# Attention's second product in one accumulation per pair of heads instead of one per query block

## The chip, the cores and the metric

The kernel runs on one core of a Trainium2 chip. The metric is the time of one execution on the device in microseconds. Three runs of the kernel before the change took 866.69, 867.77 and 871.31 us; their median is 867.77.

The engines are named as in the profile: PE is the matrix engine, PEld its weight loads, DVE the vector engine, ACT the scalar engine, POOL the general-purpose one, SP the queue that issues most DMAs.

## The reference

One layer of a hybrid trunk over 16 learned tokens and 512 input tokens of width 1024. A combined projection feeds an RWKV-7 recurrence (8 heads), a forgetting attention (8 heads, "FoX") and two gates; the two branches are gated, projected and added, and an MLP with squared ReLU follows. The change concerns the attention alone, cut here to what matters:

```python
def block(i):                                    # 128 queries
    logits = einsum('bqhd,bkhd->bhqk', qb, k) * HEAD_DIM ** -0.5
    logits = logits + (Fq[..., None] - F[:, :, None, :])     # F: running sum of log forget gates
    p = softmax(where(kpos <= qpos, logits, -inf), axis=-1)
    return einsum('bhqk,bkhd->bqhd', p, v)       # the second product
```

## The kernel before, in words

The span has three stages. To about 413 us the input projection runs in float32 parts (L501, tiles `pj`), with the recurrence and the attention beside it. From about 440 us come the output projections (L1054, L1086, L1103), then the MLP (L1133, L1251).

In the first stage several generators share PE. PE's instructions are placed in the order in which the generators issue them; a planner (`Turns`, with estimated times from `Clock`) asks each generator at every `yield` when it could go on, and lets the first by rank go that is ready. The chain of the recurrence has rank 0, the rest of the recurrence 1, `attention` 2, `fox_features` (which makes q, k, v of a pair) 3, group norm 4, and the projections, which fill what is left, 8. The other engines' instructions are ordered by a list scheduler from the dependences and from the order of the program.

`attention` takes the heads by pairs p = 0 to 3; the heads e = 0, 1 of a pair lie in the partitions 0 to 63 and 64 to 127 (`hss`). The 512 queries come in four blocks i of 128, and block i looks at the 16 meta keys and at key blocks j = 0 to i. Three steps are made for a block:

- `scored(i)`: scores on PE into PSUM (tiles `psc`, L607), mask and minimum on DVE (L616, L618), exponential with row sum on ACT (L621), division on DVE (L622, L623). The result is `pe`, queries in the partitions.
- `turned(i)`: PE transposes `pe` by key block into PSUM (`ppt`, and `ppm` for the meta keys at i = 3; L636, L638), DVE copies the key blocks to SBUF (`pT`, L640), ACT the meta keys (`pTm`, L641).
- `mixed(i)`: the second product. For each head a matmul over the meta keys (L649) opens the accumulation in the PSUM tile `py`, and one over each key block j up to i (L652) goes on with it, each with 128 queries as moving columns and 64 output rows; ACT copies the 128 x 128 result to `y_fx` (L653).

They go in the order turned(i), scored(i + 1), mixed(i). The PSUM tiles `psc`, `ppt`, `ppm`, `py` and those of the other generators take turns in four banks (`sm`). After the first stage `y_rw` (the recurrence's output) and `y_fx` are split in two float32r parts (`yhi` by ACT, `ylo` by DVE, L270 and L271), one split for each pair p, and L1054 takes them up; its PSUM pool takes over the banks of the first stage.

[...]

Of the kernel before, what the change touches and what calls it, by code (L numbers as in the profile page):

```python
# [9 lines left out]
F32 = mybir.dt.float32  # L10
# [11 lines left out]
S = 512  # L22
# [164 lines left out]
def kernel(ctx, tc, ht, x, win, par, cst, gain, lora, wout, wo, wup, wdn, out, dbg=None):  # L187
    nc = tc.nc
    dbg = dbg or {}
    mm = nc.tensor.matmul  # L190
    act = nc.scalar.activation
    V, G, A = nc.vector, nc.gpsimd, nc.scalar
# [87 lines left out]
    with ExitStack() as st:  # L280
# [8 lines left out]
        def psm(name="psm"):  # L289
            return ps.tile([128, 512], F32, name=name, tag="sm", bufs=4)  # L290
# [42 lines left out]
        with tc.tile_pool(name="xp", bufs=2) as xp:  # L333
# [14 lines left out]
            for t in range(2):  # L348
# [13 lines left out]
                n = 0  # L362
# [40 lines left out]
        y_fx = yp.tile([128, 4, S], F32, name="y_fx")  # L403
# [17 lines left out]
        fp = st.enter_context(tc.tile_pool(name="fp", bufs=1))  # L421
# [3 lines left out]
        ck = Clock(nc)  # L425
# [3 lines left out]
        def banks(n):  # L429
            return ck.ring("sm", n, 4)  # L430
# [155 lines left out]
        def attention():  # L586
            for p in range(4):
                yield fox_ready[p]
                q, k, vt, vm = fox_tiles[p]


                along = []
                for e in range(2):
                    nF = fp.tile([128, T], F32, name=f"nF{e}")
                    nc.sync.dma_start(nF, fF_d[2 * p + e:2 * p + e + 1, :].to_broadcast([128, T]))
                    along.append(nF)

                def scored(i):

                    n = NM + 128 * (i + 1)  # L600
                    parts = [(0, n)] if n <= 512 else [(0, n - 256), (n - 256, n)]
                    yield lambda: max(ck.ready(q, k), banks(2 * len(parts)))
                    scs = [[], []]
                    for a, b in parts:
                        for e, hs in enumerate(hss):
                            sc = psm("psc")[:, :b - a]
                            mm(sc, q[hs, 128 * i:128 * i + 128], k[hs, a:b], start=True, stop=True)  # L607
                            scs[e].append((sc, a, b))
                    pes = []
                    for e in range(2):  # L610
                        pe = fp.tile([128, T], F32, name="pe", bufs=2)
                        nm = fp.tile([128, 2], F32, name="nm", bufs=3)
                        least = 3e38
                        for x, (sc, a, b) in enumerate(scs[e]):
                            if b == n:
                                V.tensor_tensor(sc[:, b - a - 128:], sc[:, b - a - 128:], cmask, ALU.add)  # L616

                            V.tensor_tensor_reduce(pe[:, a:b], sc, along[e][:, a:b], -1.0, least, ALU.add, ALU.min, nm[:, x:x + 1])  # L618
                            least = nm[:, x:x + 1]
                        rsum = fp.tile([128, 1], F32, name="rsum", bufs=3)  # L620
                        act(pe[:, :n], pe[:, :n], AF.Exp, bias=least, scale=-1.0, accum_out=rsum)  # L621
                        V.reciprocal(rsum, rsum)  # L622
                        V.tensor_scalar(pe[:, :n], pe[:, :n], rsum, None, ALU.mult)  # L623
                        pes.append(pe)
                    return pes

                def turned(i, pes):

                    pTs = []
                    pTm = fp.tile([48, 128], F32, name="pTm")  # L630
                    for e in range(2):
                        pe, m = pes[e], slice(32 * e, 32 * e + 16)
                        yield lambda: max(ck.ready(pe), banks(1 + i // 3))
                        pt = psm("ppt")
                        ptm = pt[:16, 384:] if i < 3 else psm("ppm")[:16, :128]
                        nc.tensor.transpose(ptm, pe[:, :NM], ident)  # L636
                        for j in range(i + 1):
                            nc.tensor.transpose(pt[:, 128 * j:128 * j + 128], pe[:, NM + 128 * j:NM + 128 * j + 128], ident)  # L638
                        pT = fp.tile([128, 4, 128], F32, name="pT", bufs=2)
                        V.tensor_copy(pT[:, :i + 1, :].rearrange("p a b -> p (a b)"), pt[:, :128 * (i + 1)])  # L640
                        A.copy(pTm[m], ptm)  # L641
                        pTs.append((pT, pTm[m]))
                    return pTs

                def mixed(i, pTs):
                    yield lambda: max(ck.ready(vt, vm, *pTs[0], *pTs[1]), banks(1))
                    py = psm("py")[:, :128]
                    for e, hs in enumerate(hss):
                        mm(py[hs], vm[32 * e:32 * e + 16, hs], pTs[e][1], start=True, stop=False)  # L649
                    for j in range(i + 1):  # L650
                        for e, hs in enumerate(hss):
                            mm(py[hs], vt[:, j, hs], pTs[e][0][:, j, :], start=False, stop=j == i)  # L652
                    A.copy(y_fx[:, p, 128 * i:128 * i + 128], py)  # L653

                pes = yield from scored(0)
                for i in range(4):
                    pTs = yield from turned(i, pes)
                    if i < 3:
                        pes = yield from scored(i + 1)
                    yield from mixed(i, pTs)  # L660
                fox_done[p].done = True


# [345 lines left out]

        turns.add(1, recurrent())  # L1010
        turns.add(2, attention())
        turns.add(3, fox_features())
        turns.add(8, projections(24 + 16))
# [17 lines left out]
    def ppd():  # L1031
        return ps.tile([128, 512], F32, name="pd")

    with ExitStack() as st:
# [8 lines left out]
        for m in range(KB):  # L1043
            w = ahead.pop() if ahead else load_w(wout[m])
            pp = []
            for br in range(2):
# [4 lines left out]
                n = 0  # L1051
# [46 lines left out]
        for i in range(4):  # L1098
            po = ppo()
            n = 0  # L1100
# [13 lines left out]
            for j in range(2):  # L1114
                cols, kk = slice(512 * j, 512 * j + 512), slice(4 * j, 4 * j + 4)
                V.scalar_tensor_tensor(xt[:, cols], hr[:, cols], ss, gB[:, cols], ALU.mult, ALU.mult)
                pt = ppd().rearrange("p (b c) -> p b c", c=128)
# [264 lines left out]
```

## Time and profile before

| | |
|---|---|
| runs | 866.69, 867.77, 871.31 us |
| median of the runs | 867.77 us |
| profiled execution | span 866.9 us from the first to the last instruction; no longer time of this execution is listed |
| PE busy | 845.5 us in 6040 matmul passes |
| second product on PE | L652: 160 passes, 13.4 us; L649: 64 passes, 7.5 us |
| its copy on ACT | L653: 16, 4.1 us |
| mean granted clock | 0.994 |

An fp32 matmul stands as two passes in the profile, so the 112 matmuls of the second product are 224 passes. Busy times on PE add up passes that overlap: two passes on different column halves run at the same time. The distance from one group's start to the next one's start is the better measure of what a group costs, and the clock column says how much of full speed PE had.

### The profile page before, as it was taken

The page shows a single profiled execution, that of the slowest core. Times are in us where ns is not written, and L with a number is a line of the kernel's source. Part 1 is how long each engine was busy: PE and PEld are TensorE (multiplying, and loading weights), DVE is VectorE, ACT ScalarE, POOL GpSimd, SP SyncE. Part 2 cuts the span into 40 slices and gives each one's busy share as a digit, 9 for nine tenths or more (in the row PEclk, how much of TensorE's full clock was granted, in tenths as well). Part 3 has the DMA queues.
Part 4 walks back from the last instruction along what each step waited for, and adds up shares of the span by engine and source line. Part 5 has one row for each costly group of instructions (what it writes and reads, how often), then busy time and mean ns, then how long its engine had stood idle before and what let it go on. Part 6 is the DMA issues. An engine that isn't in the chain of part 4 may idle for free.

```text
span 866.9 us, 15869 instructions
## 1 busy us (share of the span) xinstructions
PE 845.5 (98%) x6040; PEld 690.8 (80%) x6040; DVE 618.4 (71%) x1222; ACT 458.0 (53%) x943; POOL 123.9 (14%) x129
## 2 busy tenths in 40 slices
PE   7899999999999999999799999999999999999998
PEld 5888887678987877778578878888888888888886
DVE  6986786658786775655767564777678777768687
ACT  7766434856566334663645453474445435534452
POOL 1112100101010000000012100202710360055000
PEclk9999999999999999999989999999999999999999
DMA  6131222121121231312356451551753184336331
GB/s 221 51 98 50 74 83 87 51 72 56 50 74 44 105 116 62 101 37 74 128 180 210 151 159 37 186 181 48 232 168 110 51 251 141 92 114 204 108 98 73
DMA packets 51340, 95.91 MB, mean 111 GB/s; under 512 B 5816, under 2 KB 6968, under 8 KB 51264
## 3 DMA queue, kind: packets, MB, share of 16 engines
q1 hardware_dynamic: 47680, 86.52, 31.8%
q0 software_dynamic: 1280, 4.20, 1.6%
q10 hardware_dynamic: 2304, 4.20, 1.3%
q8 instruction: 47, 0.77, 0.4%
q14 instruction: 29, 0.24, 0.1%
HBM read 88.57 MB, written 6.31 MB: 109 GB/s over the span
## 4 chain that ended last, share of the span: by engine, by line
PE 83%; DVE 5%; ACT 4%; DMA 2%; issue 1%; POOL 0%; ACTq 0%; DVEq 0%; POOLq 0%
PE pj L501 26%; PE po L1133 20%; PE po L1251 11%; PE pd L1251 5%; PE po L1054 3%; PE pw L841 2%; PE po L1103 2%; PE psc L607 1%; PE py L652 1%; PE psr L788 1%; PE pbt L796 1%; DMA wraw<-in_wo 1%; PE ppt L638 1%; DMA gl<-gd 1%; PE pssq L553 1%
## 5 line engine op out<-in xcount | busy, mean ns | idle before, releaser
L501 PE MATMUL pj<-uhi,whi 128*128 128x264 f32 (+1 forms) x480 | 164.9, 343 | 0.0
L501 PE MATMUL pj<-ulo,whi 128*128 128x264 f32 (+1 forms) x480 | 155.1, 323 | 2.5 <-DVE ulo L401 2.5
L501 PE MATMUL pj<-uhi,wlo 128*128 128x264 f32 (+1 forms) x480 | 154.7, 322 | 0.0
L501 PEld LDWEIGHTS pj<-uhi,whi 128*128 128x128 f32 x480 | 90.9, 189 | 17.1 <-issue 8.0
L501 PEld LDWEIGHTS pj<-ulo,whi 128*128 128x128 f32 x480 | 91.2, 190 | 7.4 <-DVE ulo L401 3.0
L501 PEld LDWEIGHTS pj<-uhi,wlo 128*128 128x128 f32 x480 | 91.1, 190 | 7.0
L1133 PE MATMUL po<-zhi,whi 128*128 128x512 f32 (+1 forms) x248 | 94.9, 383 | 0.3 <-ACT whi L235 0.3
L1133 PE MATMUL po<-zhi,wlo 128*128 128x512 f32 (+1 forms) x248 | 94.9, 383 | 0.0
L1133 PE MATMUL po<-zlo,whi 128*128 128x512 f32 (+1 forms) x248 | 94.8, 382 | 0.0
L236 DVE TENSOR_TENSOR wlo<-wraw,whi 128x512 fp32r<-128x512 f32 x88 | 72.5, 836 | 30.1 <-ACT whi L235 30.0
L235 ACT CAST whi<-wraw 128x512 fp32r<-128x512 f32 x88 | 53.7, 617 | 50.7 <-PE po L1133 23.1
L471 DVE TENSOR_TENSOR wlo<-wraw,whi 128x512 fp32r<-128x512 f32 x80 | 55.9, 705 | 25.1 <-ACT whi L470 24.3
L470 ACT CAST whi<-wraw 128x512 fp32r<-128x512 f32 x80 | 48.9, 618 | 40.6 <-PE pj L501 31.6
L270 ACT CAST whi<-t 128x512 fp32r<-128x512 f32 x64 | 39.9, 624 | 44.5 <-DVE wlo L271 20.6
L1251 PE MATMUL po<-wlo,fhi 128*128 128x512 f32 x160 | 62.8, 392 | 0.2 <-DVE wlo L271 0.2
L271 DVE TENSOR_TENSOR wlo<-t,whi 128x512 fp32r<-128x512 f32 x64 | 49.3, 784 | 19.0 <-ACT whi L270 18.1
L1251 PE MATMUL po<-whi,flo 128*128 128x512 f32 x160 | 62.4, 390 | 0.0
L1251 PE MATMUL po<-whi,fhi 128*128 128x512 f32 x160 | 61.9, 389 | 0.0
L1179 POOL TENSOR_TENSOR t<-traw 128x512 f32<-128x512 f32 x24 | 34.3, 1433 | 155.2 <-DVE wlo L271 137.9
L1133 PEld LDWEIGHTS po<-zhi,whi 128*128 128x128 f32 x248 | 46.6, 188 | 9.7 <-ACT whi L235 0.8
L1133 PEld LDWEIGHTS po<-zhi,wlo 128*128 128x128 f32 x248 | 46.6, 188 | 9.4 <-DVE wlo L236 0.4
L1133 PEld LDWEIGHTS po<-zlo,whi 128*128 128x128 f32 x248 | 46.6, 188 | 9.0
(306 smaller groups left out, 1774.6 us busy)
## 6 DMA issues: line engine op xcount, KB each, us to landing
wraw<-in_win SPq DMA_DIRECT2D x84, 256.0 KB, 2.7
wraw<-in_wup SPq DMA_DIRECT2D x64, 256.0 KB, 3.2
wraw<-in_wdn SPq DMA_DIRECT2D x48, 256.0 KB, 2.7
traw<-in_wdn SPq DMA_DIRECT2D x48, 256.0 KB, 3.0
gd<-gt ACTq DMA_DIRECT2D x16, 256.0 KB, 2.1
wraw<-in_wout SPq DMA_DIRECT2D x16, 256.0 KB, 3.1
gl<-gd SPq DMA_DIRECT2D x16, 256.0 KB, 2.8
wraw<-in_wo SPq DMA_DIRECT2D x16, 256.0 KB, 3.0
```

What stands on the lines that cost most here:

```text
L235: A.copy(hi, raw)
L236: low.tensor_tensor(lo, raw, hi.bitcast(F32), ALU.subtract)
L270: A.copy(hi, x)
L271: V.tensor_tensor(lo, x, hi.bitcast(F32), ALU.subtract)
L470: A.copy(hi, raw)
L471: low.tensor_tensor(lo, raw, hi.bitcast(F32), ALU.subtract)
L501: mm(po, a, b[:, k, a0:a1], start=n == 0, stop=n == 23)
L841: mm(ps_[hs, n - b0, :], lhs(n)[hs], rhs(n)[hs], start=True, stop=True)
L1054: mm(po, a, b[:, k, :], start=n == 0, stop=n == 11)
L1133: mm(po[:, t0:t1], a, b[:, k, t0:t1], start=n == 0, stop=n == 23)
L1179: eng.tensor_tensor(t, sums[c, pair] if c in (T1, T2) else c, d, ALU.add)
L1251: mm(x[i], a[:, k, left, 128 * i:128 * i + 128], c, start=start and k == 0 and n == 0, stop=stop and k == n_pairs - 1 and n == 2)
```

## The change

The second product is no longer made for each query block. `turned(i)` stores its transposed key blocks in a buffer that lasts for the whole pair: `pT[e]` has ten places of 128 columns, in an order that puts all queries that look at one key block side by side. Key block 0 has places 0 to 3 (queries 0 to 3), key block 1 places 4 to 6, key block 2 places 8 and 9, key block 3 place 7. The places of one query block are three apart, so DVE writes up to three of them with one strided copy; at i = 3 the fourth is copied by ACT. The meta keys go to `pTm`, which now has 512 columns.

`mixed()` runs once a pair, after `turned(3)`: for each head one matmul over the meta keys with 512 columns, then one for each key block with 512, 384, 256 and 128 columns, all into one PSUM tile, and one ACT copy of 128 x 512. It yields once behind key block 0. A pair has 10 matmuls instead of 28, with as many columns in all. [...]

```diff
+                pT = [fp.tile([128, 10, 128], F32, name=f"pT{e}") for e in range(2)]
+                pTm = fp.tile([48, S], F32, name="pTm")
...
                 def turned(i, pes):
-                    pTs = []
-                    pTm = fp.tile([48, 128], F32, name="pTm")
...
-                        pT = fp.tile([128, 4, 128], F32, name="pT", bufs=2)
-                        V.tensor_copy(pT[:, :i + 1, :].rearrange("p a b -> p (a b)"), pt[:, :128 * (i + 1)])
-                        A.copy(pTm[m], ptm)
-                        pTs.append((pT, pTm[m]))
-                    return pTs
+                        pt = pt.rearrange("p (a b) -> p a b", b=128)
+                        n = min(i + 1, 3)
+                        V.tensor_copy(pT[e][:, i:i + 3 * n - 2:3, :], pt[:, :n, :])
+                        A.copy(pTm[m, 128 * i:128 * i + 128], ptm)
+                        if i == 3:
+                            A.copy(pT[e][:, 7, :], pt[:, 3, :])
 
-                def mixed(i, pTs):
-                    yield lambda: max(ck.ready(vt, vm, *pTs[0], *pTs[1]), banks(1))
-                    py = psm("py")[:, :128]
+                def mixed():
+                    yield lambda: max(ck.ready(vt, vm, pTm, *pT), banks(1))
+                    py = psm("py")
                     for e, hs in enumerate(hss):
-                        mm(py[hs], vm[32 * e:32 * e + 16, hs], pTs[e][1], start=True, stop=False)
-                    for j in range(i + 1):
+                        mm(py[hs], vm[32 * e:32 * e + 16, hs], pTm[32 * e:32 * e + 16, :], start=True, stop=False)
+                    for j, at in enumerate((0, 4, 8, 7)):
                         for e, hs in enumerate(hss):
-                            mm(py[hs], vt[:, j, hs], pTs[e][0][:, j, :], start=False, stop=j == i)
-                    A.copy(y_fx[:, p, 128 * i:128 * i + 128], py)
+                            mm(py[hs, 128 * j:], vt[:, j, hs], pT[e][:, at:at + 4 - j, :].rearrange("p a b -> p (a b)"), start=False, stop=j == 3)
+                        if j == 0:
+                            yield lambda: 0.0
+                    A.copy(y_fx[:, p, :], py)
 
                 for i in range(4):
-                    pTs = yield from turned(i, pes)
+                    yield from turned(i, pes)
                     if i < 3:
                         pes = yield from scored(i + 1)
-                    yield from mixed(i, pTs)
+                yield from mixed()
...
-    nc = bacc.Bacc("TRN2", target_bir_lowering=False, num_devices=1)
+    nc = bacc.Bacc("TRN2", target_bir_lowering=False, num_devices=1, dynamic_dma_scratch_size=8192)
```

Lines move with it: the meta-key matmul L649 becomes L651, the key-block matmul L652 becomes L654, the copy L653 becomes L657, the scores L607 become L609, the exponential L621 becomes L623, the output projection L1054 becomes L1058.

What the order of the instructions shows, at three places. On PE, in the first pair, before: the block of i = 3 among the steps of the recurrence's chain (`pch`, `pyy`, `pvt`).

```order
908 L907 MATMUL pch<-Rs,Tt 64x64 x4
909 L887 MATMUL pvt<-cs,ov 128x64 x2
910 L649 MATMUL py<-pTm,vm 64x128 x2
911 L652 MATMUL py<-pT,vt 64x128 x8
912 L922 MATMUL pch<-uv,bkT 64x64 x4
```

After, in the same pair:

```order
895 L651 MATMUL py<-pTm,vm 64x512 x2
896 L654 MATMUL py<-pT_1502,vt 64x512
897 L654 MATMUL py<-pT_1503,vt 64x512
898 L905 MATMUL pch<-uv,L_703 64x64
899 L905 MATMUL pch<-uv,L_704 64x64
900 L905 MATMUL pch<-uv,L_1121 64x64
901 L905 MATMUL pch<-uv,L_1122 64x64
902 L654 MATMUL py<-pT_1502,vt 64x384
903 L654 MATMUL py<-pT_1503,vt 64x384
904 L654 MATMUL py<-pT_1502,vt 64x256
905 L654 MATMUL py<-pT_1503,vt 64x256
906 L654 MATMUL py<-pT_1502,vt 64x128
```

The one block of the pair is cut in two by a step of the chain; the blocks of i = 0 to 2 further up are gone. The second and third pair are cut in the same way, by L841 and by L922 to L933; the fourth is not cut.

On PE, at the end of the first stage, fourth pair, before:

```order
2160 L649 MATMUL py<-pTm,vm 64x128 x2
2161 L652 MATMUL py<-pT,vt 64x128 x6
2162 L636 MATMUL ppm<-cs,pe 16x128
2163 L638 MATMUL ppt<-cs,pe 128x128 x4
2164 L636 MATMUL ppm<-cs,pe 16x128
2165 L638 MATMUL ppt<-cs,pe 128x128 x4
2166 L649 MATMUL py<-pTm,vm 64x128 x2
2167 L652 MATMUL py<-pT,vt 64x128 x8
2168 L1054 MATMUL po<-yhi,whi 128x512
```

After:

```order
2161 L636 MATMUL ppm<-cs,pe 16x128
2162 L638 MATMUL ppt<-cs,pe 128x128 x4
2163 L651 MATMUL py<-pTm,vm 64x512 x2
2164 L654 MATMUL py<-pT_5255,vt 64x512
2165 L654 MATMUL py<-pT_5256,vt 64x512
2166 L654 MATMUL py<-pT_5255,vt 64x384
2167 L654 MATMUL py<-pT_5256,vt 64x384
2168 L654 MATMUL py<-pT_5255,vt 64x256
2169 L654 MATMUL py<-pT_5256,vt 64x256
2170 L654 MATMUL py<-pT_5255,vt 64x128
2171 L654 MATMUL py<-pT_5256,vt 64x128
2172 L1058 MATMUL po<-yhi,whi 128x512
```

The three earlier blocks have left the places between the transposes, and the whole pair's product stands between the last transpose and the next stage.

On ACT, at the same place, before (casts of `y_rw` and `y_fx`, and the exponential of 528 columns, which is that of i = 3):

```order
418 L641 COPY pTm<-ppt 16x128
419 L270 CAST yhi<-y_rw 128x512 x2
420 L641 COPY pTm<-ppt 16x128
421 L270 CAST yhi<-y_rw 128x512 x2
422 L270 CAST yhi<-y_fx 128x512
423 L621 ACTIVATE pe,rsum<-pe,nm 128x528 x2
424 L653 COPY y_fx<-py 128x128
425 L270 CAST yhi<-y_fx 128x512 x2
```

After:

```order
414 L270 CAST yhi<-y_rw 128x512 x2
415 L642 COPY pTm<-ppt 16x128
416 L270 CAST yhi<-y_rw 128x512 x2
417 L642 COPY pTm<-ppt 16x128
418 L270 CAST yhi<-y_fx 128x512 x3
419 L623 ACTIVATE pe,rsum<-pe,nm 128x528 x2
420 L642 COPY pTm<-ppm 16x128 x2
421 L644 COPY pT_5255<-ppt 128x128
422 L644 COPY pT_5256<-ppt 128x128
423 L657 COPY y_fx<-py 128x512
```

Two more casts stand ahead of the last exponential, and two copies of the fourth key block behind it. On DVE, four splits of `y_rw` stand ahead of the last division (L623 before, L625 after) in both kernels, and one of `y_fx` only after.

## The prediction

> **What bounds the kernel now.** I read the page first, then stretches of the span, then the chain of waits and the timeline around the second product.
>
> ```profile
> span 866.9 us, 15869 instructions
> ...
> 115.00:413.00 298.00, 296.54 (x3094) 235.57 (x3093) 201.26 (x533) 161.59 (x406) 13.86 (x18) 1.00 0.23 73
> 413.00:434.00 21.00, 16.11 (x113) 10.46 (x111) 17.35 (x62) 15.66 (x45) 0.00 (x0) 1.00 0.41 141
> 434.00:442.00 8.00, 7.18 (x37) 5.43 (x38) 4.91 (x10) 2.21 (x7) 0.00 (x0) 0.57 0.43 159
> ```
>
> The last three rows are stretches: start and end, length, busy time of PE, PEld, DVE, ACT and POOL, then the granted clock. Attention for the first three pairs lies in 115 to 413 us, where PE is idle for 1.5 of 298 us: projections (L501) fill every gap, so PE time taken out there should shorten the span one for one. The fourth pair lies in 413 to 440 us. The projections run out there, PE is idle a quarter of the time, and from 434 us the clock falls to 0.57. There the path is a chain, read from the chain of waits (start, length, what):
>
> ```profile
> 428.40 1.38 PE psc L607 x5
> ...
> 430.48 1.66 ACT yhi L270 x3
> 432.14 0.74 ACT pe L621 x2
> ...
> 433.06 0.59 DVE ylo L271
> ...
> 434.13 0.59 DVE ylo L271
> ...
> 436.42 0.62 PE py L649 x4
> ...
> 439.21 0.27 ACT y_fx L653
> ...
> 439.53 6.67 PE po L1054 x24
> ```
>
> The last block's exponential (L621) starts behind casts of y_rw and y_fx that stand ahead of it on ACT, DVE splits stand between its steps, and the next stage (L1054) waits for the last product's copy out of PSUM. So the change acts at two places with two prices.
>
> **Front: the product in the three pairs under cover of projections.** One block each of i = 0, 1, 2, 3, with what PE did next (timeline: start, length, what; four passes stand for two matmuls, since each fp32 matmul is two):
>
> ```profile
> 339.01 0.43 PE L649 MATMUL py<-pTm,vm 16*64 16x128 f32 x4
> 339.37 0.44 PE L652 MATMUL py<-pT,vt 128*64 128x128 f32 x4
> 339.74 1.33 PE L870 MATMUL pw<-Tt,W 32*32 32x32 f32 x72
> ...
> 252.44 0.43 PE L649 MATMUL py<-pTm,vm 16*64 16x128 f32 x4
> 252.81 0.66 PE L652 MATMUL py<-pT,vt 128*64 128x128 f32 x8
> 253.40 0.39 PE L501 MATMUL pj<-uhi,whi 128*128 128x264 f32 x1
> 253.62 0.28 PE L501 MATMUL pj<-ulo,whi 128*128 128x264 f32 x1
> 253.74 0.29 PE L501 MATMUL pj<-uhi,wlo 128*128 128x264 f32 x1
> ...
> 357.64 0.43 PE L649 MATMUL py<-pTm,vm 16*64 16x128 f32 x4
> 358.01 0.88 PE L652 MATMUL py<-pT,vt 128*64 128x128 f32 x12
> 358.71 0.40 PE L901 MATMUL pch<-uv,L 128*64 128x64 f32 x8
> ...
> 179.59 0.43 PE L649 MATMUL py<-pTm,vm 16*64 16x128 f32 x4
> 179.96 1.09 PE L652 MATMUL py<-pT,vt 128*64 128x128 f32 x16
> 180.88 0.40 PE L922 MATMUL pch<-uv,bkT 128*64 128x64 f32 x8
> ```
>
> From the first start to the next group's start: 0.73, 0.96, 1.07 and 1.29 us, 4.05 us a pair. Between i = 0 and i = 1 four passes of 128 columns add 0.23 us, with the same kind of entry, so a pass costs 55 to 57 ns; the 56 passes of a pair are 56 x 0.055 = 3.08 us, and the rest, about 0.29 us a block with 8 passes (0.73 - 8 x 0.055), is the change of tile shape. Leaving a block costs the neighbour too: the first projection after it takes 0.22 us to the next start, later ones 0.12, so 0.1 us more, and I put entry at the same.
>
> The new block streams as many columns in fewer, longer passes: four of 512 (meta keys), then four each of 512, 384, 256 and 128. The nearest row for a long pass is a 64 by 64 product of 512 columns, and what followed it:
>
> ```profile
> 74.18 1.02 PE L553 MATMUL pssq<-fsq,cs 64*64 64x512 f32 x4
> 75.13 0.39 PE L501 MATMUL pj<-uhi,whi 128*128 128x264 f32 x1
> ```
>
> 0.95 us with the exit, 0.85 without it: 213 ns a pass, which is 53 ns for 128 columns. So a pair's streaming is 8 x 0.213 + 4 x (0.160 + 0.107 + 0.053) = 2.99 us. One block's shape change (0.29) makes 3.28; the new block also yields once behind its first 512-wide key block, and in the three pairs something stands in that place, for which I add 0.15: about 3.4. Gain per pair 4.05 - 3.4 = 0.65, plus entry and exit at 0.1 each for two places fewer (four become two) = 0.4. Three pairs: **-3 us**. Ends: 0, if PE waits for something else after all, and -4.4, if nine blocks' whole overhead goes (9 x (0.29 + 0.2)).
>
> [...]
>
> **The tail: the fourth pair.** Its three earlier blocks ran where PE waited for DVE anyway, so their removal gives nothing; their work, 36 of the 56 column units, moves to the end. Three terms.
>
> First, the queues. With fewer things waiting on y_fx, three casts of it stand ahead of the last exponential, where one stood, and one more DVE split stands ahead of the last multiply. A cast cost 0.55 us in the chain (1.66 / 3) and a split 0.59: +1.1 us on ACT, and DVE's 0.59 runs partly beside it. Against that, y_rw's last multiply is moved ahead of a multiply, so its casts can begin up to 0.4 us sooner. I take +0.9; ends 0 and +1.7 (1.1 + 0.59).
>
> Second, the product. Before, its last block took 2.79 us (436.42 to 439.21) at the low clock:
>
> ```profile
> 434.00:436.00 2.00, 1.53 (x10) 1.29 (x10) 2.00 (x6) 1.18 (x4) 0.00 (x0) 0.68 0.90 367
> 436.00:438.00 2.00, 2.00 (x15) 1.34 (x16) 1.87 (x4) 0.00 (x0) 0.00 (x0) 0.50 0.02 8
> ...
> 440.00:442.00 2.00, 2.00 (x7) 1.55 (x7) 0.69 (x1) 0.26 (x2) 0.00 (x0) 0.61 0.79 262
> ```
>
> From the 0.68 and the 0.61 the clock was halved from about 434.7 to 441.6 us. If it lasts as long in the changed kernel, the block starts at 436.4 + 0.9 = 437.3, does 4.3 us at half speed, that is 2.1 of its 3.28, and the other 1.15 at full: it ends at 442.75.
>
> Third, the copy: it has 512 columns instead of 128. The nearest row of that shape is the copy of vt:
>
> ```profile
> L578 ACT COPY vt<-pv x4: 569/586/588, 114.8 to 413.6; 128x512 f32<-128x512 f32 x4
> ```
>
> 0.59 for the 0.27 of the chain, so L1054 starts at 443.4 instead of 439.5, 3.9 us late. It then runs at full clock, where before it lost half of 439.5 to 441.6, 1.0 us. The tail: **+2.9 us**. Ends: +0.6 if no half clock comes (ready 0.9 later, 3.28 for 2.79, +0.32, -1.0 for L1054), and +4.5 if it stays through the block (3.28 x 2 = 6.6 us, and L1054 saves half of what it lost).
>
> [...] Here it closed behind an idle piece of 2.4 us:
>
> ```profile
> 430.51 0.43 PE L649 MATMUL py<-pTm,vm 16*64 16x128 f32 x4
> 430.88 0.88 PE L652 MATMUL py<-pT,vt 128*64 128x128 f32 x12
> 434.12 0.28 PE L636 MATMUL ppm<-cs,pe 128*16 128x128 f32 x1 [2.37 <-DVE pe L623]
> ```
>
> With the block of i = 2 gone (430.5 to 431.8 us) that piece grows to 3.6 us or more, so I count on a closed gate. [...]
>
> What costs nothing: two more 128-column ACT copies a pair and 12 copies of y_fx fewer leave ACT, busy 161.6 of 298 us in the front, about as it was; in the tail the copies of the fourth key block are wanted only by the last two matmuls, behind 3 us of streaming. The DVE copies of pT write as many columns as before, in blocks, and the last leaves 128 of its 512 to ACT. [...]
>
> ```profile
> L1170 POOL DMA_DIRECT2D traw<-in_wdn x16: 536/536/707, 537.3 to 564.6; - x16
> ...
> traw<-in_wdn POOLq DMA_DIRECT2D x16, 256.0 KB, 3.2
> ```
>
> Sum: -3.0 + 2.9 = -0.1 us on a span of 866.9. No longer time of the profiled execution is listed; the three runs are 866.69, 867.77 and 871.31, so I set it against the median: 867.7.
>
> **Rivals.** (a) Slower by the clock: with three blocks out of the stretch 413 to 434 us PE is busy some 13 of 21 us instead of 16, and the gate may close before the last scores are made. It decides once it closes before the scores of i = 2:
>
> ```profile
> 422.35 0.27 PE L636 MATMUL ppt<-cs,pe 128*16 128x128 f32 x1 [1.12 <-ACT yT L963]
> ...
> 423.55 0.94 PE L607 MATMUL psc<-ka,qa 64*128 64x400 f32 x4
> ```
>
> Those scores then cost 0.9 us more, those of i = 3 1.4 (the 1.38 of the chain), the transposes 0.3, the product 6.6 instead of 5.45 and L1054 up to 1.7. That is +5.4 on the forecast, 873.1. For it: a 2.37 us gap sufficed once. Against it: the gap of 1.12 us left the clock at 1.00.
>
> (b) Faster by weight loads: a pair has 20 loads instead of 56, 144 fewer in all.
>
> ```profile
> L652 PEld LDWEIGHTS py<-pT,vt 128*64 128x64 f32 x160 | 9.4, 145 | 2.9 <-issue 2.9
> ```
>
> If half of a load stood between the passes, 144 x 0.07 = 10 us would go, less the tail's 2.9: 861. Against it, passes follow each other in 55 ns, well under one load. [...]
>
> (c) The tail is covered or the gate stays open: -3 + 0.6 = 865.4, no measurable change. (d) The small scratch makes POOL's loads wait for one another, 3.2 us each: 16 x 3.2 = 51 us for what now takes 27, and DVE's sums hold up the splits: up to +20, 887.
>
> **How the numbers follow.** About 0.5%, 4.3 us, is what a measurement of this kernel can tell from no change: under 863.4 or over 872.1. Forecast 0.59, (c) 0.17, (a) 0.12, (b) 0.06, (d) 0.02; 0.04 is left for the new order of the projections, half each way. The forecast's terms span -4.4 + 0.6 to 0 + 4.5, so it and (c) stay inside but for 0.02 on the fast side. Faster 0.10, same 0.74, slower 0.16. The range takes in the ends -3.7 and +4.5: 864.0 to 872.3.
>
> **What would show it.** L651 and L654 together near 3.3 us a pair in the front; PE time in the front down by 3 us; three y_fx casts ahead of the last L623 exponential; the last block 5 us or more with a clock of 0.5; L1058 starting no earlier than L1054 did. I am wrong if the gate opens early or closes before the last scores, or if the front gives much more than 4 us.

## The result and the profile after

The changed kernel takes 870.98 us (median of 19 runs, 868.48 to 875.63); the kernel before took 867.45 in 19 runs beside it. The ratio is 1.0046 [1.0033, 1.0058]: slower by about 4 us, where 867.7 and no measurable change were forecast.

The profiled execution of after is one of its fastest runs:

```profile
span 867.0 us, 15565 instructions
...
PE 842.1 (97%) x5896; PEld 683.1 (79%) x5896; DVE 620.2 (72%) x1222; ACT 458.3 (53%) x939; POOL 123.8 (14%) x129
```

It took 868.78 us, 1.8 us of them around the span. So the two profiles differ by 0.1 us, while the medians differ by 3.5. The profiles show where time moved; how much is lost on the whole must come from the medians.

The same three stretches as before:

```profile
115.00:413.00 298.00, 295.14 (x2997) 231.85 (x2996) 199.46 (x535) 162.57 (x407) 13.86 (x18) 1.00 0.23 73
413.00:434.00 21.00, 12.89 (x62) 8.10 (x61) 17.45 (x56) 14.56 (x37) 0.00 (x0) 0.79 0.51 176
434.00:442.00 8.00, 7.59 (x26) 2.84 (x24) 1.99 (x4) 1.12 (x4) 0.00 (x0) 0.50 0.00 0
```

The granted clock in 413 to 434 us is 0.79 where it was 1.00, and from 434 to 442 us it is 0.50. PE's records show 7.59 of those 8 us busy, at half speed. Cut finer, along the steps of 3.41 us in which the clock changes (last section):

```profile
414.98:418.39 3.41, 1.68 (x12) 1.12 (x11) 3.38 (x14) 3.34 (x10) 0.00 (x0) 1.00 0.41 130
418.39:421.80 3.41, 3.41 (x12) 1.55 (x13) 2.57 (x8) 1.38 (x4) 0.00 (x0) 0.50 0.50 157
421.80:425.21 3.41, 1.01 (x10) 0.77 (x8) 3.05 (x12) 2.06 (x6) 0.00 (x0) 1.00 0.23 77
425.21:428.63 3.42, 3.42 (x15) 2.07 (x13) 2.52 (x7) 3.15 (x8) 0.00 (x0) 0.50 0.76 241
428.63:432.04 3.41, 0.66 (x3) 0.25 (x2) 3.18 (x12) 2.76 (x7) 0.00 (x0) 1.00 1.01 389
432.04:435.45 3.41, 2.51 (x12) 2.06 (x14) 3.41 (x9) 0.78 (x3) 0.00 (x0) 0.50 0.15 61
435.45:438.87 3.42, 3.42 (x10) 0.58 (x8) 0.54 (x2) 0.27 (x1) 0.00 (x0) 0.50 0.00 0
438.87:442.28 3.41, 2.73 (x14) 1.14 (x10) 0.00 (x0) 0.59 (x1) 0.00 (x0) 0.50 0.00 0
```

The clock is halved three times, from about 418.4 (3.4 us), 425.2 (3.4 us) and 432.0 us (10.2 us), each time behind a step of which PE's records fill half or less (1.68, 1.01 and 0.66 of 3.41 us). PE's next work starts within 1 us of each closing, and so runs at half clock. The timeline shows the gaps; the number ahead of the arrow is PE's idle time before the instruction:

```profile
418.32 0.34 PE L636 MATMUL ppt<-cs,pe 128*16 128x128 f32 x1 [1.73 <-DVE pe L625]
...
424.99 0.28 PE L636 MATMUL ppt<-cs,pe 128*16 128x128 f32 x1 [2.40 <-DVE pe L625]
...
432.94 0.37 PE L636 MATMUL ppm<-cs,pe 128*16 128x128 f32 x1 [3.65 <-DVE rsum L624]
```

The chain of waits through the same place:

```profile
409.17 0.44 PE pv L577 x4
...
419.86 1.64 PE psc L609 x4
...
426.82 2.02 PE psc L609 x6
...
433.31 0.85 PE ppt L638 x4
...
435.23 1.90 PE py L651 x4
437.13 4.52 PE py L654 x16
...
441.67 0.60 ACT y_fx L657
...
442.31 3.70 PE po L1058 x15
```

The fourth pair's work (L577, `pv`) starts at 409.17 us instead of 413.08, and the next stage (L1058) at 442.31 instead of 439.53. In between lie 33.1 us instead of 26.4. Both scores (1.64 and 2.02 us) and the whole product (1.90 + 4.52 us) run at half clock.

### The profile page after: what moved, and what is told of

Read it like the earlier page. It is cut to its first block, busy times and chain, and to the rows that moved or that the text cites. A ratio compares the mean times of both kernels' runs of the same rounds, so it can differ in the third digit from the quotient of the medians.

```text
span 867.0 us, 15565 instructions
## 1 busy us (share of the span) xinstructions
PE 842.1 (97%) x5896; PEld 683.1 (79%) x5896; DVE 620.2 (72%) x1222; ACT 458.3 (53%) x939; POOL 123.8 (14%) x129
## 4 chain that ended last, share of the span: by engine, by line
PE 88%; DVE 5%; ACT 2%; issue 1%; DVEq 0%; ACTq 0%
PE pj L501 25%; PE po L1137 20%; PE po L1255 12%; PE po L1058 5%; PE pd L1255 5%; PE po L1107 3%; PE pw L845 2%; PE psc L609 1%; PE py L654 1%; PE pd L1090 1%; PE po L1090 1%; PE pbt L800 1%; PE psr L792 1%; PE ppt L638 1%; PE pch L911 1%
```

## The experiments

For each run of a kernel its mean granted clock is listed; I work out the half-clock time as (1 - clock) x 2 x span and give the mean over a kernel's runs. Where the prediction speaks of a clock gate that is closed or open, the measured thing is the granted clock: at half, or in full. All kernels compute the whole reference. Each ratio is taken to the runs of before beside the same kernel; their medians are 867.45 beside after, 867.54 beside e5 to e8 and 868.10 beside e9 and e10.

| kernel | median us | runs | ratio to before | half clock, mean us |
|---|---|---|---|---|
| before (the 32 runs beside e1 to e4) | 867.43 | 32 | 1 | 11.4 |
| after | 870.98 | 19 | 1.0046 [1.0033, 1.0058] | 24.0 |
| e1: old product in the last pair only | 867.72 | 12 | 0.9995 [0.9975, 1.0016] | 13.6 |
| e2: new product in the last pair only | 872.23 | 9 | 1.0054 [1.0037, 1.0072] | 22.8 |
| e3: after, gaps filled | 864.58 | 12 | 0.9969 [0.9953, 0.9985] | 4.8 |
| e4: before, `dynamic_dma_scratch_size=8192` | 867.22 | 12 | 1.0000 [0.9981, 1.0020] | 12.4 |
| e5: before, gaps filled | 864.31 | 11 | 0.9961 [0.9945, 0.9976] | 4.1 |
| e6: e1, gaps filled | 862.79 | 7 | 0.9948 [0.9929, 0.9968] | 4.4 |
| e7: after, casts moved | 871.19 | 6 | 1.0040 [1.0024, 1.0056] | 22.0 |
| e8: after, gaps filled with projections | 864.85 | 12 | 0.9966 [0.9949, 0.9982] | 6.5 |
| e9: after, early gaps filled | 868.96 | 11 | 1.0009 [0.9996, 1.0022] | 14.2 |
| e10: after, late gap filled | 868.75 | 11 | 1.0017 [1.0000, 1.0035] | 15.9 |

### One part alone: e1 and e2

e1 keeps the change in the first three pairs and makes the last pair's product per query block, as before, out of the new buffers. e2 does the reverse.

```diff
+                def mixed_block(i):
+                    ...
+                    py = psm("py")[:, :128]
+                    for e, hs in enumerate(hss):
+                        mm(py[hs], vm[...], pTm[32 * e:32 * e + 16, 128 * i:128 * i + 128], start=True, stop=False)
+                    for j, at in list(enumerate((0, 4, 8, 7)))[:i + 1]:
+                        for e, hs in enumerate(hss):
+                            mm(py[hs], vt[:, j, hs], pT[e][:, at + i - j, :], start=False, stop=j == i)
+                    A.copy(y_fx[:, p, 128 * i:128 * i + 128], py)
...
-                yield from mixed()
+                    if p == 3:                  # e2: p < 3
+                        yield from mixed_block(i)
+                if not (p == 3):                # e2: p < 3
+                    yield from mixed()
```

> Pairs 0 to 2 take the new product, pair 3 again one block per query block (with the new buffers and the new copies); scratch 8192. Theory (the front gains about 4 us, and the tail loses more because PE's clock is halved for longer): the front's gain stays and the tail is as before, so about 863.5 us, 4 faster than before, with the clock halved for about 7 us in the tail and nothing ahead of it. Rival 1 (the loss comes from the new buffers, the strided copies or the scratch): still 868 or more. Rival 2 (the front gains nothing, what the two profiles show is chance): 867.5, as before.

> The reverse: pairs 0 to 2 one block per query block, pair 3 the new product. Theory: the whole loss without the gain, 4 us above the changed kernel, about 874.5 us, with the clock halved more than once between 410 and 445 us. Rival 1 (loss from buffers, copies or scratch everywhere): about 871. Rival 2: as before, 867.5.

e2 came as slow as after (872.23, some 2 us less than expected), so the last pair carries the loss. In e2 the clock is down there as well:

```profile
420.00:430.00 10.00, 5.91 (x27) 3.35 (x27) 8.69 (x27) 6.35 (x19) 0.00 (x0) 0.79 0.43 134
430.00:445.00 15.00, 11.08 (x40) 5.38 (x41) 8.10 (x24) 6.62 (x16) 0.00 (x0) 0.57 0.39 140
```

e1 was a miss: the loss is gone, but no gain shows. The expected gain had been read off two profiles, before's and after's, and these differ in something that is not the change: before's has a half-clock piece at about 42 us (0.93 in 36 to 60 us), after's has none (1.00 there). e1's own profile has more of them, and its tail is at half clock for 10.2 us (433.8 to 444.0), where about 7 were expected:

```profile
36.00:60.00 24.00, 21.51 (x149) 19.90 (x151) 19.98 (x36) 16.67 (x31) 6.85 (x9) 0.86 0.22 74
...
145.00:165.00 20.00, 18.38 (x290) 14.87 (x290) 10.06 (x26) 13.84 (x35) 0.95 (x2) 0.91 0.04 15
```

Runs of one kernel differ in this too: the mean clock of the 32 runs of before beside e1 goes from 0.988 to 0.998, which is some 21 to 3.5 us of half clock. A single profile of each kernel can't give a gain of 3 us as long as they differ by such pieces.

### The clock kept at full: e3 and e5

To see whether the clock makes the loss, PE gets idle work in the gaps of the last pair: products of `uhi` with itself, into a projection bank that nobody reads. Put ahead of the transposes of i = 1, 2 and 3, they number 7, 9 and 14 in after (e3), and 4, 3 and 10 in before (e5), whose gaps are smaller. They add work, so what they save must come from something else that they change. One such thing is the clock. Another is an order: with products ahead of the transposes of i = 3, all casts and splits of `y_rw` and `y_fx` come behind the last exponential and the last division (e3, e5, e6, e8 and e10), while before and after have most of them ahead of these. So e3 and e5 alone don't separate the clock from this order; e9 and e10 below do.

```diff
                 yield ...                      # turned(i), ahead of the transposes
+                        if p == 3 and e == 0 and i > 0:
+                            warm = ppj("pj")
+                            for _ in range((0, 7, 9, 14)[i]):        # e5: (0, 4, 3, 10)
+                                mm(warm, uhi[:, 0, :128], uhi[:, 1, :512], start=True, stop=True)
```

> The changed kernel with idle matmuls that nobody reads (7, 9 and 14 of 128 x 128 by 512, about 0.23 us each) placed on PE ahead of the transposes of i = 1, 2, 3 of pair 3, where PE waits for DVE. Theory (the halved clock is the loss): the clock stays at 1.00 in the tail, the scores and the last product run at full speed, and the time falls to 863 to 864 us. Rival 1 (the loss is the casts and splits that now stand ahead of the last exponential, and the longer last product itself): the clock stays up but the time falls by 2 us at most, 869. Rival 2 (the fillers delay the transposes): slower than 871.

> The kernel before with 4, 3 and 10 idle matmuls of 512 columns ahead of the transposes of i = 1, 2, 3 of pair 3, sized to the idle pieces of its own tail (1.1, 0.8 and 2.4 us). Theory (a halved clock costs about 0.4 us for each us that it lasts): its mean of 11 us at half clock falls to about 5, and the time by 2 to 2.5 us, to 865; the changed kernel's loss against before would then be nothing but a longer stay at half clock. Rival (the fillers act in some other way in the changed kernel, for example by moving the order of the transposes): no gain here, 867.5 or more.

In both the granted clock is 1.00 from 410 to 445 us. The stretches of e3:

```profile
410.00:420.00 10.00, 9.33 (x55) 6.86 (x54) 6.63 (x28) 7.20 (x22) 0.00 (x0) 1.00 0.20 65
420.00:430.00 10.00, 9.43 (x49) 6.56 (x50) 9.13 (x32) 5.16 (x15) 0.00 (x0) 1.00 0.32 96
430.00:445.00 15.00, 14.29 (x70) 9.76 (x70) 9.43 (x16) 10.62 (x20) 1.38 (x1) 1.00 0.68 246
```

After gains 6.4 us (870.98 to 864.58), before only 3.2 (867.54 to 864.31). At full clock there the two kernels stand at 0.9969 and 0.9961: 0.3 us apart by the medians, 0.7 by the ratios, with some 1.9 us of uncertainty. So at full clock, and with the casts and splits at the end in both, the change does nothing that can be measured, and the difference of the two gains, 3.2 us, is most of its loss of 3.5 to 4 us.

These two profiles can be compared step by step, since each has one half-clock piece at about 40 us and no other before the last 2 us. Chain of waits of e3 (product now L656, L659; copy L662; next stage L1063):

```profile
410.09 0.44 PE pv L577 x4
...
432.21 1.72 PE py L656 x4
433.93 2.35 PE py L659 x16
436.31 0.59 ACT y_fx L662
...
436.95 10.27 PE po L1063 x44
```

Of e5:

```profile
413.17 0.44 PE pv L577 x4
...
437.56 0.17 ACT y_fx L658
...
437.78 9.37 PE po L1059 x40
```

The front: `pv` starts 3.1 us sooner (410.09 against 413.17). The tail, from `pv` to the next stage: 26.9 us against 24.6, so 2.2 longer. The net at the next stage is -0.8 us, and not all of that reaches the end. PE's one wait between 500 and 536 us is `pd` (L1119 in before) for DVE's `xt`: 1.1 us in before, 0.6 in e5, 1.3 in e3. The chain of waits of e3 leads to that `xt` from a weight load, through casts and sums on ACT and DVE, not from the first stage:

```profile
497.20 4.72 DMA wraw<-in_wo
...
511.44 0.76 DVE xt L1125
...
512.25 0.66 PE pd L1128 x4
```

So e3, which comes 0.8 us earlier than e5, waits 0.7 us longer there. (Before comes later than both and waits 1.1 us, so the time of arrival alone doesn't set the wait.) After doesn't wait there at all: 1.1 us of the 2.8 by which its next stage starts later are given back there.

### Which gap: e9 and e10

e9 fills only the gaps of i = 1 and 2 (7, 9, 0 products), e10 only that of i = 3 (0, 0, 14).

> The changed kernel with idle matmuls ahead of the transposes of i = 1 and 2 alone (7 and 9), none ahead of i = 3, where PE waits longest (3.65 us). If the half clock that costs most is the late one, over the last transposes and the last product: only a part of the 6.4 us of all fillers comes back, 868 to 869, with the clock halved from about 432 us. If the early windows over the scores of i = 2 and 3 cost most: 865 to 866.

> The changed kernel with 14 idle matmuls ahead of the transposes of i = 3 alone. If the late half clock costs most: 866 to 867, with the clock halved at times between 415 and 428 us and at 1.00 in the last product. If the early windows cost most: 868 to 869.

By the ratios e9 gives back 3.2 us of after's time, e10 2.5, both together (e3) 6.7: within their uncertainty of 1.6 to 1.9 us each the parts add up, and neither is the cause alone. In e9 the clock is halved from 429.6 to 439.8 us. In e10 the clock fell to half at 418.5 us and stayed there until 432:

```profile
418.00:432.00 14.00, 10.90 (x38) 7.01 (x39) 10.91 (x37) 6.21 (x18) 0.00 (x0) 0.52 0.30 94
```

Two pairs of runs differ in the clock while ACT and DVE keep their order in the last pair: after and e9 (casts ahead of the last exponential), e10 and e3 (casts behind it). By the ratios e9 is 3.2 us faster than after, with 9.8 us less of half clock, and e3 is 4.2 us faster than e10 (with 2.1 us of uncertainty), with 11.2 us less. That is 0.33 and 0.37 us for each us at half clock. The 12.6 us that after has more than before are then worth 4 to 5 us: the clock alone is enough for the loss of 3.5 to 4 us, whatever the order does. What the front gains comes on top (about 2 us, see below), so 1 to 2 us are left for the longer last product and copy; no run measures that rest by itself.

### The casts: e7

The forecast's first term was the order on ACT: more casts of `y_fx` ahead of the last exponential. e7 ties them behind it.

```diff
-                        act(pe[:, :n], pe[:, :n], AF.Exp, bias=least, scale=-1.0, accum_out=rsum)
+                        last_exp[0] = act(pe[:, :n], pe[:, :n], AF.Exp, bias=least, scale=-1.0, accum_out=rsum)
...
-                split(yhi[:, 4 * j + k, :], ylo[:, 4 * j + k, :], src[:, k, :])
+                a_ = A.copy(yhi[:, 4 * j + k, :], src[:, k, :])
+                if j == 1:
+                    after(a_, last_exp[0])
+                V.tensor_tensor(ylo[:, 4 * j + k, :], src[:, k, :], yhi[:, 4 * j + k, :].bitcast(F32), ALU.subtract)
```

> The changed kernel, with the four casts of y_fx kept behind the last exponential on ACT, so that they no longer stand ahead of it. The prediction's first term of the tail (casts and splits ahead of the last exponential, +0.9 us): 870. Theory (that wait is not on the path, DVE's splits and the half clock are): 871, no change.

Nothing: 871.19 (1.0040 [1.0024, 1.0056]) beside after's 1.0046. The casts of `y_fx` were not on the path of after. ACT's timeline of after had said so:

```profile
428.07 1.66 ACT L270 CAST yhi<-y_fx 128x512 fp32r<-128x512 f32 x3
429.95 0.74 ACT L623 ACTIVATE pe<-pe,nm 128x528 f32<-128x528 f32 x1 [0.22 <-DVE nm L620]
```

The exponential waited 0.22 us for DVE's minimum behind the casts, since the scores at half clock came late enough for the casts to be done. At full clock it is otherwise. e9 keeps after's order, and its clock is full from 410 to 429.6 us; there the exponential follows the casts at once, 19.2 us behind `pv` (410.34 us):

```profile
427.99 1.66 ACT L270 CAST yhi<-y_fx 128x512 fp32r<-128x512 f32 x3
429.56 0.73 ACT L623 ACTIVATE pe<-pe,nm 128x528 f32<-128x528 f32 x1
```

In e3 the casts stand behind it, and it starts 18.3 us behind `pv`:

```profile
428.35 0.74 ACT L623 ACTIVATE pe<-pe,nm 128x528 f32<-128x528 f32 x1 [1.39 <-DVE nm L620]
```

That is 1.0 us, though DVE's splits are moved as well.

### The scratch: e4

e4 is before with `dynamic_dma_scratch_size=8192` alone, a setting that before leaves out.

> The kernel before with the descriptor scratch of 8192 bytes alone. Theory: 867.5, no change, and the 16 POOL loads land in about 3.2 us as before. Rival (the loads wait for one another): 869 or more, and longer landing times.

867.22, ratio 1.0000 [0.9981, 1.0020]. POOL's loads land as fast as before's 3.2 us:

```profile
traw<-in_wdn POOLq DMA_DIRECT2D x16, 256.0 KB, 3.1
```

### Towards a better kernel: e6 and e8

e6 is e1 with 4, 3 and 10 idle products; e8 is after with the 24 matmuls of the last gate's projection held back and spread 6, 9 and 9 over the three gaps, so that useful work fills them.

```diff
+                if p == 3:
+                    _, hw = convert(*fetch((9, 0, B_GATE + 15)))     # the gate's weights
...
+                            for k_ in ((), (0, 1), (2, 3, 4), (5, 6, 7))[i]:
+                                for n_, (a, b) in enumerate(passes(wk(hw, k_), U)):
+                                    mm(hpo[0], a, b[:, k_, NM:T], start=k_ == 0 and n_ == 0, stop=k_ == 7 and n_ == 2)
...
-        turns.add(8, projections(24 + 16))
+        turns.add(8, projections(24 + 15))
```

> Pairs 0 to 2 with the new product, pair 3 with one block per query block, and the same 4, 3 and 10 idle matmuls. Theory (the front gains 2 us, which the run of pairs 0 to 2 alone hid behind its spread): 863, 2 below the kernel before with the same fillers. Rival (the front gains nothing): 865, like the kernel before with fillers.

> The changed kernel with real work in place of the idle matmuls: the projection of the last gate (24 matmuls of 512 columns, 5.5 us) is taken out of the stretch before pair 3 and stands in three parts (6, 9, 9) ahead of the transposes of i = 1, 2, 3 of pair 3. Theory: the clock stays up as with the fillers (864.6) and the stage before is shorter by up to 5.5 us: 860. Rival (the gate's copy, its conversion and its transfer delay ACT and DVE in the tail, where DVE is busy all the time): 863 to 865, no better than the fillers.

e6 is the fastest, 862.79: 0.9948 [0.9929, 0.9968], quicker than both kernels. Its chain of waits has the front's gain without the tail's loss:

```profile
410.42 0.44 PE pv L577 x4
...
435.47 11.63 PE po L1077 x50
```

The tail is 25.0 us, `pv` starts 2.7 us sooner than in e5. Of these only 1.5 us show in the medians of e6 and e5 (862.79, 864.31), and 0.6 in their profiled spans (862.4, 863.0), in part because e6 waits 1.3 us for `xt` where e5 waits 0.6. Whether the front alone is worth 1.5 or nearer 3 us, the runs don't settle: the intervals overlap.

e8 takes 864.85 where 860 was expected, no better than idle products, though its 24 matmuls no longer stand ahead of the last pair. Its timeline says where they went:

```profile
412.79 1.65 PE L614 MATMUL psc<-ka,qa 64*128 64x272 f32 x4
...
434.01 0.50 PE L1073 MATMUL po<-yhi,whi 128*128 128x512 f32 x1 [1.23 <-ACT whi L235]
```

The same scores take 1.00 us at full clock: with no projection left behind the first scores, the clock was at half there (0.83 in 410 to 420 us, that is 3.4 us of half clock). And the next stage, 434.01 us, waits for its weights: by the chain of waits their load (`wraw<-in_wout`, 5.90 us, landing at 434.4) was issued only behind the held matmuls.

## Why the prediction was wrong, point by point

**The failed step** is the sentence "If it lasts as long in the changed kernel". The half-clock piece of before, 434.7 to 441.6 us, was carried over as it stood. It began earlier and came three times: 17 us of half clock between 418 and 442 us in the profile of after, 7 in that of before; 24.0 against 11.4 as means of the runs. From `pv` to the next stage after takes 6.7 us longer than before (33.1 against 26.4), where the three terms made 3.9. That is rival (a), given 0.12. Its condition was met (closed at 418.4, ahead of 423.55), at the gap it had used as evidence against itself: 1.12 us before, and 1.73 with the block of i = 0 gone from it. Its price of 873 was 2 us high: the scores of i = 3 took 2.02 us in the chain, not 1.38 + 1.4, as the clock came back to full at 428.65 us, during them; the product took 6.42 (priced 6.6).

**The front, -3 us:** the sign and the mechanism held; the size is nearer 2. `pv` starts 3.1 (e3) and 2.7 us (e6) sooner than in e5, but e5 is the latest of its kind. Of the nine profiles with just one half-clock piece of 3.4 us ahead of it and the gate's projection in its place, four have the old product in the front (before, e2, e4, e5: 412.1 to 413.2 us) and five the new one (e3, e6, e7, e9, e10: 409.8 to 411.6 us). The means are 412.7 and 410.4, 2.2 us apart. The block took what was forecast; first pair of after:

```profile
173.65 1.07 PE L651 MATMUL py<-pTm,vm 16*64 16x512 f32 x4
174.66 1.08 PE L654 MATMUL py<-pT,vt 128*64 128x512 f32 x4
175.57 0.40 PE L905 MATMUL pch<-uv,L 128*64 128x64 f32 x8
175.80 1.47 PE L654 MATMUL py<-pT,vt 128*64 128x384 f32 x12
177.19 0.45 PE L911 MATMUL pch<-Rs,Tt 64*64 64x64 f32 x8
```

From start to start 1.01 + 0.91 + 1.39 = 3.31 us, where 3.28 and 0.15 for the cut were put. That the 0.29 us a block in the 3.28 go with the change of tile shape is seen in the rows of before alone: past 55 ns a pass, the next row starts 0.15 us later where its shape differs (i = 0 and 1), and 0.04 where it is 128*64 as well (i = 2 and 3). The four long passes take 0.91 / 4 = 228 ns with the exit.

**The tail's first term, +0.9 for the casts:** not there in after; e7 shows nothing. The term added lengths of queued work without asking whether the exponential's other input, DVE's minimum, came later still, as it did behind scores at half clock. At full clock the term is there: 1.0 us between e9 and e3, splits included.

**The product and the copy:** at full clock the change makes the tail 2.2 us longer (e3 against e5). The forecast's end for that case, +0.6, set the new product against before's at half clock, so it can't be compared with this directly; its own terms (0.9 + 0.49 + 0.32 - 1.0) make 0.7. The product's two rows in e3 take 4.07 us, not 3.28: the four 512-column passes over the meta keys stand with 1.72 us against 1.01 in the front. There the weights of the second head wait for ACT's copy of `pTm`, which stands behind a cast:

```profile
432.86 0.19 PEld L656 LDWEIGHTS py<-pTm,vm 16*64 16x64 f32 x2 [0.53 <-ACT pTm L647]
```

So the passes of the two heads, side by side in the front, run one after the other. This comes from the order in e3, where the casts stand at the end: in after the same row takes 1.90 us at half clock, less than twice 1.01. The copy took 0.59 and 0.60, as forecast.

**L1058 at full clock, -1.0:** the clock was back at 1.00 from 442.3 us, so this held. What the forecast did not see is the wait for `xt` near 512 us, which gives back another 1.1 us of a late tail.

**Rivals (b) and (d)** are out: the long passes took no less for their columns than the short ones (228 ns with the exit for 512 columns, 55 for 128), and e4 shows the setting of the scratch to cost nothing (867.22 us, loads landing in 3.1 us). No run shows what the scratch holds. (By its own numbers, 51 us for 27, (d) was 24 us, not up to 20.) Rival (c), -2.4 us without the half clock, is not what e3 against e5 shows either: +0.3 to +0.7 us, with 1.9 of uncertainty.

**The reading of the profile** that would have told: the row of 413 to 434 us had PE busy 16 of 21 us at clock 1.00 and 7 us at half clock right behind it. The change takes three blocks of 0.73, 0.96 and 1.07 us, 2.8 us of PE work, out of just this stretch. I priced that work at nothing, because PE waited for DVE anyway; but without it the clock fell, in e2 as well, where the last pair alone is changed (22.8 us of half clock a run, 11.4 in before).

## What to carry to other kernels

Here a stretch had PE waiting (16 of 21 us busy) and the clock at half behind it, and 2.8 us of PE work in it were not free to remove: the half clock rose from 11.4 to 24.0 us a run. In such a stretch ask what the gaps become, and price the slower case over all that PE does until it is busy again. Idle products in the gaps are a cheap test of whether the clock makes a loss: here they gave 3.2 us in one kernel and 6.4 in the other. But look at what else they move: here the scheduler put the casts and splits elsewhere, and only runs of equal order (after and e9, e10 and e3) show the clock by itself. And a change that is good in one place and bad in another is better made per place: the new product in the covered pairs and the old one in the last, with the gaps filled, is the best version found (862.79 us).

## What the runs showed of the hardware

In the profile of before the clock is at half from 42.20 us (3.41 us long) and from 434.73 (6.83), in that of after from 418.41 (3.41), 425.24 (3.41) and 432.06 (10.24), beside a last piece at the end of each trace. In each of the two these changes lie whole multiples of 3.41 us apart; in before, from 45.61 to 434.73 us, it is 114 of these steps. Cut along the steps from 12 to 855 us, where the clock is full, the two profiles show four steps with 0.66 to 1.04 us of PE's records (before: 1.00 and 1.04; after: 1.01 and 0.66); each was followed by half clock. So was one with 1.68 us, in after (414.98 to 418.39), though PE's longest idle piece in it was 1.73 us. One with 1.62 us in after (36.12 to 39.54) was not, nor one with 2.00 us in before (421.04 to 424.45), nor any of the 478 others, which have 2.3 us or more.

PE's records alone don't tell when the clock comes back to full. In e10 it stayed at half for 13.7 us, while PE's records fill 10.9 of the 14 us from 418 to 432, and in after it stayed at half behind a step that the records fill wholly (435.45 to 438.87 us).

Eleven of the twelve profiles have half clock between 36 and 60 us (a granted clock of 0.93 there, 0.86 in e1), in a stretch that the change does not touch; after's has none (1.00). Within a kernel, runs with more half-clock time are longer by 0.26 to 0.46 us for each us of it (kernels with nine runs or more); this is part of the spread from 863.21 to 871.31 us that before shows.
